# A written order for the mixer's projection on three engines, with x loaded ahead, a fifth gate tile as block products and forms moved behind the attention

## The chip, the cores and the metric

The kernel runs on one core of a Trainium2 chip. A core has TensorE (PE, matrix products into PSUM banks), VectorE (DVE), ScalarE (ACT), GpSimd (POOL), and DMA queues, of which the kernel uses SyncE's (SP) for nearly all loads and POOL's for loads that add to what is in the buffer. The metric is the device time of one execution in microseconds (us); the median of three runs counts.

## The reference

One layer on x of 512 x 1024 in float32. `D` is 1024, the tiles of 128 channels are numbered m or k.

```python
h = rms_norm(x, norm_mix)
q_a, k_a, v_a, u_b, gate_b, gate_c, g_a, g_b = jnp.split(h @ w_in, split_points, axis=-1)
o_a = stick_breaking_attention(heads(q_a), heads(k_a), heads(v_a))
y_b = gate_b * causal_depthwise_conv(gate_c * u_b, conv_w)
merged = sigmoid(g_a) * (o_a @ w_branch_a) + sigmoid(g_b) * (y_b @ w_branch_b)
x = x + merged @ w_mix_out
x = x + memory_cross_attention(rms_norm(x, norm_mem_q), rms_norm(mem, norm_mem_kv), ...)
gate, up = jnp.split(rms_norm(x, norm_ffn) @ w_ffn_in, 2, axis=-1)
x = x + (silu(gate) * up) @ w_ffn_out
return rms_norm(x, norm_final)
```

The change touches the sixth line from its gates on, and the seventh, with what the memory attention's query (memory-q) needs of its result.

## The kernel before

All activations lie transposed, channels on partitions and 512 positions along the row. Each float32 product is made of three products in a faster type: every operand is split into a high part, a cast on ACT (`wh`, `mh`, names ending in h), and a low part, a subtraction on DVE (`wl`, `ml`), and `mm3` issues high x high, high x low and low x high. A weight tile goes through `load_w`: a 512 KB load by SP into a buffer of the tag `wr`, the cast to `wh` on ACT, the subtraction to `wl` on DVE. **The tag `wr` has four buffers**, and so has each of `wh` and `wl`.

The larger weights are computed as seven *block products* in place of eight half products (`product(ps, m, i)`, i = 0 to 6, each with 12 matmuls 256 columns wide). Those need sums of weight blocks, which `ffn_load` makes: `ws` (a 512 KB load, then an accumulating load on POOL's queue), `wg` (512 KB) and `a22` (256 KB). `ws` and `wg` take buffers of the tag `wr` too, but for one of them at two of three tiles, which take the tag `wg` of another pool. `ffn_raw` adds further sums, `ffn_form` splits one into high and low (`wf`). On the side of the activations each pair of tiles is turned into *forms*: `xf`, `xo`, `xc`, `xd` with h and l behind, by `forms_of`, where c and d are differences of blocks.

The stages from about 150 us on:

- *Attention.* The stick-breaking attention on PE, ACT, DVE and POOL, its order left to the scheduler.
- *Gates, branches.* For each tile m the two gates (projections of h, a sigmoid each) and the two branch projections (`branch`: 12 + 12 matmuls into a bank `br`, each multiplied by its gate in place on DVE, then added to the merged tile `m`). In tiles 0 to 3 the gates are direct (24 matmuls, 512 wide, each); the last `GATES` = 4 tiles use block products, whose x forms are built pair by pair by `pair_load` and `pair_forms` (an xp load of 512 KB into a `wr` buffer, two scalings by ACT at line 776, then the sums). The last tiles run under a written order on PE, ACT and DVE: products by number, and at each the reads of its bank (`gate_reads`), the form of a product four ahead, the sum of one six ahead, and at i = 6 the branch. `gate_second` adds the second half of a gate; for the last tile it stands behind the product i = 5. `merged.append(split(...))` makes `mh` and `ml` of the merged tiles.
- *Mixer.* `residual(wmix_d, ...)`: for m = 0 to 7 one block of 24 matmuls (512 wide) into a bank `r`, drawn from two banks that `br` and `v` use as well; then the load of x (SP, 256 KB, line 622), the add x <- r + x (DVE, L625), the scaled `xr` (ACT, L628), at odd m the forms of the pair, and the squares for the next norm. Nothing sets the order here but the scheduler's priorities and the buffers.
- *Memory-q.* Block products again: `z`, `v`, `y` banks, in a written order whose head takes products 0 to 2 over the first three pairs first, then the fourth pair, then i = 3, 4 and so on.
- *The second residual* (`wmo_d`) and the FFN use the same code and forms.

SP carries out its loads in program order: a load whose buffer is not free holds those behind it.

Of the kernel before, what the change touches and what calls it, by code (L numbers as in the profile page):

```python
# [13 lines left out]
P = 128  # L14
D = 1024
S = 512
# [16 lines left out]
QM = NF + NB  # L33
GATES = 4
GM = QM + D // (2 * P)
# [12 lines left out]
def hybrid_layer(ctx: ExitStack, tc: tile.TileContext, xT_d, memT_d, cols_d, wv_d, win_d,  # L48
# [540 lines left out]

    def forms_of(xe, xo):  # L590

        b11 = xe[:, :HS]
        c, d = sums_of(xe, xo)
        u = unit("xf")
        nc.scalar.copy(u[:, :HS], b11)
        nc.vector.tensor_tensor(out=u[:, HS:], in0=b11, in1=f(u[:, :HS]), op=ALU.subtract)  # L596
        (oh, ol), (ch, cl), (dh, dl) = split(xo, "xo"), split(c, "xc"), split(d, "xd", new=spare)
        return listed((u[:, :HS], u[:, HS:]), oh, ol, ch, cl, dh, dl)

# [5 lines left out]
    def residual(w_dram, act, old, gain):  # L605


        xs, xn = [], []
        acc = tmp("acc")
        ps, w, even = {}, {}, {}  # L610

        def block(m, k0, k1, bank=mmtile):
            if k0 == 0:
                w[m] = load_w(w_dram[m])
# [3 lines left out]
            if k1 < KD:  # L618
                return
            if old is None:  # L620
                xm = f(unit("x"))
                nc.sync.dma_start(xm, xT_d[m * P:(m + 1) * P, :])
            else:
                xm = old[m]
            nc.vector.tensor_tensor(out=xm, in0=ps[m], in1=xm, op=ALU.add)  # L625
            xs.append(xm)
# [12 lines left out]

        return (xs, xn, acc), block  # L640

# [5 lines left out]

    raws, pairs = {}, {}

    def ffn_load(m):  # L650
# [101 lines left out]

    def branch(m, sig, w):
        for j, a in ((1, yb), (0, oT)):
            ps = mmtile("br")
            gemm(ps, w, a, 4 * j)
            nc.vector.tensor_tensor(out=sig[j], in0=ps, in1=sig[j], op=ALU.mult)
        t = f(spare("m"))
# [14 lines left out]
    def pair_forms(k2, xp):  # L773
        for j in range(2):
            k = 2 * k2 + j
            nc.scalar.activation(xp[:, j, :], xp[:, j, :], AF.Copy, scale=g_mix[:, k:k + 1])
# [4 lines left out]
    x0f = []  # L781
    for m in range(KD - GATES):
        sig = []
        for j in range(2):
# [3 lines left out]
            squash(sig[j])  # L788
        if m < KD // 2:
            xp = pair_load(m)  # L790
        branch(m, sig, load_w(wbr_d[m]))
        if m < KD // 2:
            x0f.append(pair_forms(m, xp))

# [34 lines left out]
    with tc.manual_schedule(engines={mybir.EngineType.PE, mybir.EngineType.Activation,  # L829
                                     mybir.EngineType.DVE}):  # L830
        wb, last_m = {}, GM + GATES - 1
        for n, (m, i) in enumerate(gs):
            product(bank_of(m, i), m, i)
            if i == 1 and m > GM:
                gate_second(m - 1)
            elif (m, i) == (last_m, 5):
                gate_second(m)
            gate_reads(m, i)
            if n + GATE_AHEAD < len(gs):
# [3 lines left out]
            if i == 3:  # L843
                wb[m] = load_w(wbr_d[KD - GATES + m - GM])
            if i == 6:
                b = banks.pop(m)
                branch(KD - GATES + m - GM, (b["g"], b["t"]), wb[m])
                sigmoid = b["sigmoid"]
            if m == last_m and i in (1, 2, 3, 4):
                merged.append(split(raw_m[len(merged)], "m"))  # L850
        while len(merged) < KD:
            merged.append(split(raw_m[len(merged)], "m"))

    (x1, x1f, acc1), mix = residual(wmix_d, merged, None, g_q)
# [127 lines left out]

    x2, last = residual(wmo_d, om, x1, g_ffn)
    with tc.manual_schedule(engines={mybir.EngineType.PE}):
# [117 lines left out]
    for k in range(TURN):  # L1102
# [3 lines left out]
        if k > 1 and k % 2 == 0 and len(af) < NT:  # L1106
            j = TURN + 2 * len(af)
            af.append(forms_of(act[j], act[j + 1]))
        for m in range(KD):
# [194 lines left out]
```

## Time and profile before

| | us |
|---|---|
| median of three runs (859.42 to 861.13) | 860.27 |
| the profiled execution | 858.25 |
| its span, first to last instruction | 856.4 |
| PE busy | 843.1 |
| DVE busy | 671.3 |
| ACT busy | 479.9 |
| POOL busy | 81.5 |

The mean granted clock of PE was 0.996 of full speed. In a row of the timeline stand the start in us from the span's start, the duration, the engine, the line, the operation, what is written from what with its shape, and in brackets how long the engine had been idle and what it waited for. A matmul's duration overlaps its neighbours'; what counts is the distance of starts. A row of waits reads: who waited, for whom, us in total, how often, the longest. A row of windows gives the stretch, its length, the busy share and count of PE, PE's weight loads, DVE, ACT and POOL, then the granted clock, the DMA share and GB/s.

### The profile page before, as it was taken

The page shows a single profiled execution, that of the slowest core. Times are in us where ns is not written, and L with a number is a line of the kernel's source. Part 1 is how long each engine was busy: PE and PEld are TensorE (multiplying, and loading weights), DVE is VectorE, ACT ScalarE, POOL GpSimd, SP SyncE. Part 2 cuts the span into 40 slices and gives each one's busy share as a digit, 9 for nine tenths or more (in the row PEclk, how much of TensorE's full clock was granted, in tenths as well). Part 3 has the DMA queues.
Part 4 walks back from the last instruction along what each step waited for, and adds up shares of the span by engine and source line. Part 5 has one row for each costly group of instructions (what it writes and reads, how often), then busy time and mean ns, then how long its engine had stood idle before and what let it go on. Part 6 is the DMA issues. An engine that isn't in the chain of part 4 may idle for free.

```text
span 856.4 us, 13976 instructions
## 1 busy us (share of the span) xinstructions
PE 843.1 (98%) x5344; PEld 762.5 (89%) x5344; DVE 671.3 (78%) x1169; ACT 479.9 (56%) x866; POOL 81.5 (10%) x106
## 2 busy tenths in 40 slices
PE   9999999999999999999999999999999999999997
PEld 7878787788899887899988889999999999888997
DVE  8769889888666967778865789888888878876864
ACT  7556766676344655566664666555554456652444
POOL 1011112111100001000000110111111110010002
PEclk9999999999999999999999999999999999999999
DMA  8332232217544745546332336777777775362312
GB/s 296 129 118 77 96 106 78 89 50 218 150 121 126 215 146 155 135 134 236 124 104 94 106 79 174 200 183 181 182 179 184 185 192 172 135 153 67 97 38 99
DMA packets 50483, 119.98 MB, mean 140 GB/s; under 512 B 5104, under 2 KB 9200, under 8 KB 50416
## 3 DMA queue, kind: packets, MB, share of 16 engines
q1 hardware_dynamic: 40880, 100.97, 36.1%
q0 software_dynamic: 9248, 17.83, 12.8%
q8 instruction: 42, 0.69, 0.3%
q10 hardware_dynamic: 288, 0.29, 0.1%
q14 instruction: 25, 0.20, 0.1%
HBM read 115.89 MB, written 2.10 MB: 138 GB/s over the span
## 4 chain that ended last, share of the span: by engine, by line
PE 90%; DVE 4%; issue 2%; DMA 2%; ACT 1%; POOL 0%; SPq 0%; DVEq 0%; POOLq 0%
PE z L706 22%; PE y L706 11%; PE v L706 5%; PE pr L162 5%; PE pr L164 5%; PE pr L163 5%; PE f L162 3%; PE f L163 3%; PE f L164 3%; PE v L268 3%; PE r L162 3%; PE r L163 3%; PE r L164 2%; PE br L163 2%; PE br L162 2%; PE br L164 2%
## 5 line engine op out<-in xcount | busy, mean ns | idle before, releaser
L157 ACT CAST wh<-wr 128x1024 fp32r<-128x1024 f32 x82 | 85.7, 1049 | 58.6 <-issue 9.7
L158 DVE TENSOR_TENSOR wl<-wr,wh 128x1024 fp32r<-128x1024 f32 x82 | 101.1, 1236 | 22.2 <-ACT wh L157 21.7
L706 PE MATMUL z<-xdh,wf 128*128 128x256 f32 x544 | 108.8, 284 | 0.0
L706 PEld LDWEIGHTS z<-xdh,wf 128*128 128x128 f32 x544 | 89.3, 191 | 0.3
L162 PE MATMUL pr<-xgh,wh 128*128 128x512 f32 x224 | 87.7, 391 | 0.0
L163 PE MATMUL pr<-xgl,wh 128*128 128x512 f32 x224 | 87.4, 390 | 0.0
L164 PE MATMUL pr<-xgh,wl 128*128 128x512 f32 x224 | 87.3, 390 | 0.0
L706 PE MATMUL z<-xdl,wf 128*128 128x256 f32 x272 | 77.1, 283 | 0.0
L730 ACT COPY sa<-z 128x256 f32<-128x256 f32 x52 | 19.4, 373 | 86.4 <-PE z L706 86.3
L697 DVE TENSOR_TENSOR wf<-s,wf 128x512 fp32r<-128x512 f32 x68 | 46.8, 689 | 24.5 <-ACT wf L696 23.3
L696 ACT CAST wf<-ws 128x512 fp32r<-128x512 f32 x68 | 41.8, 618 | 32.3 <-PE r L163 10.0
L688 DVE TENSOR_TENSOR wf<-wg,wf 128x1024 fp32r<-128x1024 f32 x34 | 41.6, 1224 | 21.4 <-ACT wf L687 21.3
L663 POOL DMA_DIRECT2D ws<-in_w_ffn_in_dram x22 | 26.5, 1203 | 306.0 <-DMA ws<-in_w_ffn_in_dram 133.1
L697 DVE TENSOR_TENSOR wf<-ws,wf 128x512 fp32r<-128x512 f32 x68 | 46.9, 690 | 10.8 <-ACT wf L696 10.7
L706 PE MATMUL y<-xch,wf 128*128 128x256 f32 x272 | 54.6, 282 | 0.0
L706 PE MATMUL z<-xch,wf 128*128 128x256 f32 x272 | 54.5, 283 | 0.0
L706 PEld LDWEIGHTS z<-xdl,wf 128*128 128x128 f32 x272 | 52.0, 191 | 0.2
L696 ACT CAST wf<-s 128x512 fp32r<-128x512 f32 x68 | 42.3, 622 | 15.5 <-DVE s L674 14.8
L706 PE MATMUL z<-xf,wf 128*128 128x256 f32 x360 | 48.9, 284 | 1.4 <-DVE xf L596 0.9
L164 PEld LDWEIGHTS pr<-xgh,wl 128*128 128x128 f32 x224 | 42.0, 188 | 8.8
L162 PEld LDWEIGHTS pr<-xgh,wh 128*128 128x128 f32 x224 | 42.1, 188 | 8.6 <-DVE rv L131 0.3
L163 PEld LDWEIGHTS pr<-xgl,wh 128*128 128x128 f32 x224 | 42.1, 188 | 8.3
(327 smaller groups left out, 2453.3 us busy)
## 6 DMA issues: line engine op xcount, KB each, us to landing
wr<-in_w_in_dram SPq DMA_DIRECT2D x28, 512.0 KB, 3.5
ws<-in_w_ffn_in_dram SPq DMA_DIRECT2D x22, 512.0 KB, 4.0
ws<-in_w_ffn_in_dram POOLq DMA_DIRECT2D x22, 512.0 KB, 6.0
wg<-in_w_ffn_in_dram SPq DMA_DIRECT2D x22, 512.0 KB, 4.5
wr<-in_w_ffn_out_dram SPq DMA_DIRECT2D x14, 512.0 KB, 3.5
a<-in_w_ffn_in_dram SPq DMA_DIRECT2D x22, 256.0 KB, 4.8
wr<-in_w_branch_dram SPq DMA_DIRECT2D x8, 512.0 KB, 3.9
wr<-in_w_mix_out_dram SPq DMA_DIRECT2D x8, 512.0 KB, 5.0
```

Source lines behind the costliest of these rows:

```text
L157: after(nc.scalar.copy(h2, raw), lead[-1:])
L158: lows.append(nc.vector.tensor_tensor(out=l2, in0=raw, in1=f(h2), op=ALU.subtract))
L162: nc.tensor.matmul(ps, a[0], b[0], start=start, stop=False, **kw)
L163: nc.tensor.matmul(ps, a[0], b[1], start=False, stop=False, **kw)
L164: nc.tensor.matmul(ps, a[1], b[0], start=False, stop=stop, **kw)
L268: nc.tensor.matmul(vps[t], xg[k][a][:, sl], wv[k][b], start=k == 0 and (a, b) == (0, 0), stop=k == KD - 1 and a == 1)
L663: nc.gpsimd.dma_start(s13, a[:, 0:4:3, :], accum_op=ALU.add)
L688: nc.vector.tensor_tensor(out=lo, in0=pair, in1=f(hi), op=ALU.subtract)
L696: nc.scalar.copy(hi, raw)
L697: nc.vector.tensor_tensor(out=lo, in0=raw, in1=f(hi), op=ALU.subtract)
L706: nc.tensor.matmul(ps[:, :HS], a, b, start=i < 3 and k == 0 and j == 0, stop=k == KP - 1 and j == 2, skip_group_check=True)
L730: nc.scalar.copy((s[:, :HS], None, None, s[:, HS:], t[:, :HS], t[:, :HS])[i], z)
```

## The change

- `GATES` goes from 4 to 5: the fourth direct gate tile becomes block products. The pair forms are made one after each of three direct branches, the fourth with the third.
- The scalings in `pair_forms` are tied behind the attention's exponentials.
- `forms_of` is cut into `even_forms` (what needs the even tile alone) and `odd_forms`, which write the same forms in another order; the residuals and the FFN use them.
- The mixer's projection comes under the written order on PE, ACT and DVE, 24 matmuls to a block; the weight of m + 2 is asked for before the last matmuls of block m, and its cast and subtraction stand there. The weight of m = 0 is asked for at the last gate tile's product 5.
- The eight loads of x are written at the last gate tile's product 6, and the `ws` loads that follow are tied behind them.
- The last gate tile's `gate_second` goes from i = 5 to i = 4. Its branch takes splits of merged tiles, and the weight of m = 1, between its matmuls and its mults (`also`).
- Memory-q's raw weights are asked for ahead of the mixer, and six of its forms are made within it, at m = 5, 6 and 7.

```diff
-GATES = 4
+GATES = 5
...
+    def even_forms(xe):
+        u, c = unit("xf"), f(unit("c1"))
+        nc.scalar.copy(u[:, :HS], xe[:, :HS])
+        nc.vector.tensor_tensor(out=c[:, :HS], in0=xe[:, :HS], in1=xe[:, HS:], op=ALU.subtract)
+        nc.vector.tensor_tensor(out=u[:, HS:], in0=xe[:, :HS], in1=f(u[:, :HS]), op=ALU.subtract)
+        return u, c, xe
+
+    def odd_forms(u, c, xe, xo):
...
+        nc.scalar.copy(ch, c)
+        nc.vector.tensor_tensor(out=ol, in0=xo, in1=f(oh), op=ALU.subtract)
...
+        nc.scalar.copy(dh, d)
+        nc.vector.tensor_tensor(out=cl, in0=c, in1=f(ch), op=ALU.subtract)
+        nc.vector.tensor_tensor(out=dl, in0=d, in1=f(dh), op=ALU.subtract)
...
+        def finish(m):
+            xm = old[m]
             nc.vector.tensor_tensor(out=xm, in0=ps[m], in1=xm, op=ALU.add)
...
             if m % 2:
-                xn.append(forms_of(even.pop(m - 1), raw))
+                xn.append(odd_forms(*even.pop(m - 1), raw))
             else:
-                even[m] = raw
+                even[m] = even_forms(raw)
...
-        nc.sync.dma_start(s13, a[:, 2:3, :].broadcast_to([P, 2, 512]))
+        after(nc.sync.dma_start(s13, a[:, 2:3, :].broadcast_to([P, 2, 512])), x_loads[-1:])
...
-    def branch(m, sig, w):
+    def branch(m, sig, w, also=()):
         for j, a in ((1, yb), (0, oT)):
             ps = mmtile("br")
             gemm(ps, w, a, 4 * j)
+            for g in also[j:j + 1]:
+                g()
             nc.vector.tensor_tensor(out=sig[j], in0=ps, in1=sig[j], op=ALU.mult)
...
-            nc.scalar.activation(xp[:, j, :], xp[:, j, :], AF.Copy, scale=g_mix[:, k:k + 1])
+            after(nc.scalar.activation(xp[:, j, :], xp[:, j, :], AF.Copy,
+                                       scale=g_mix[:, k:k + 1]), exps[-2:])
...
+            if (m, i) == (last_m, 4):
                 gate_second(m)
...
+            if (m, i) == (last_m, 5):
+                mix_all, mix, mix_w = residual(wmix_d, merged, x1, g_q)
+                mix_w(0)
             if i == 6:
+                if m == last_m:
+                    for k in range(KD):
+                        x1.append(f(unit("x")))
+                        x_loads.append(nc.sync.dma_start(x1[k], xT_d[k * P:(k + 1) * P, :]))
                 b = banks.pop(m)
-                branch(KD - GATES + m - GM, (b["g"], b["t"]), wb[m])
+                branch(KD - GATES + m - GM, (b["g"], b["t"]), wb[m],
+                       (lambda: (merge(1), mix_w(1)), lambda: merge(2)) if m == last_m else ())
...
-    for m in range(KD):
-        mix(m, 0, KD)
-
-    qs = order(QM, MH)
-    for n in range(AHEAD + SUM_AHEAD):
-        ffn_raw(*qs[n], nc.gpsimd)
-    for n in range(AHEAD):
-        ffn_form(*qs[n])
+        qs = order(QM, MH)
+        for n in range(AHEAD + SUM_AHEAD):
+            ffn_raw(*qs[n], nc.gpsimd)
+        for m in range(KD):
+            mix(m, 0, KD - 1)
+            if m + 2 < KD:
+                mix_w(m + 2)
+            mix(m, KD - 1, KD)
+            for n in {5: (0, 2), 6: (3, 4), 7: (5,)}.get(m, ()):
+                ffn_form(*qs[n])
```

Three places show how the engines' orders move. First SP's queue, at the mixer's weights, before (`wr` from in_w_mix_out are the mixer's weights, `ws`, `wg` and `a` memory-q's):

```order
L150 DMA wr_3164<-in_w_mix_out_dram 128x1024
L662 DMA a_3525<-in_w_mem_q_dram 128x512
L150 DMA wr_3224<-in_w_mix_out_dram 128x1024
L150 DMA wr_3263<-in_w_mix_out_dram 128x1024
L150 DMA wr_3323<-in_w_mix_out_dram 128x1024
L150 DMA wr_3362<-in_w_mix_out_dram 128x1024
L150 DMA wr_3422<-in_w_mix_out_dram 128x1024
L150 DMA wr_3461<-in_w_mix_out_dram 128x1024
L622 DMA x_3158<-in_xT_dram 128x512
L658 DMA ws_3521<-in_w_mem_q_dram 128x2x512
```

and with the change:

```order
L150 DMA wr_3203<-in_w_mix_out_dram 128x1024
L681 DMA a_3220<-in_w_mem_q_dram 128x512
L883 DMA x_3148<-in_xT_dram 128x512
L883 DMA x_3162<-in_xT_dram 128x512
L677 DMA ws_3216<-in_w_mem_q_dram 128x2x512
L677 DMA ws_3225<-in_w_mem_q_dram 128x2x512
L679 DMA wg_3227<-in_w_mem_q_dram 128x1024
L677 DMA ws_3705<-in_w_mem_q_dram 128x2x512
L681 DMA a_3229<-in_w_mem_q_dram 128x512
L150 DMA wr_3254<-in_w_mix_out_dram 128x1024
L150 DMA wr_3294<-in_w_mix_out_dram 128x1024
L150 DMA wr_3347<-in_w_mix_out_dram 128x1024
```

(six more loads of x stand between the two shown). Before, all eight weights of the mixer stood ahead of x and of most of memory-q's raws; now those of m = 2 to 7, from wr_3254 on, stand behind them, and `ws_3216`, `ws_3225` and `wg_3227` are in buffers of the tag `wr`.

Second, DVE at the end of the last gate tile and the start of the mixer, with the change (`sb` and `fg` are the gates, `br` the branch banks, `m` the merged tiles):

```order
L836 SCALAR_TENSOR_TENSOR sb_2924<-z_2923,r0b_338 128x256
L158 TENSOR_TENSOR wl_3130<-wr_3127,wh_3129 128x1024
L840 TENSOR_TENSOR fg_2937<-y_2982,fg_2937 128x256
L841 TENSOR_TENSOR fg_2937<-fg_2937,r0b_338 128x512
L177 TENSOR_TENSOR ml_3178<-m_2731,mh_3177 128x512
L177 TENSOR_TENSOR ml_3182<-m_2899,mh_3181 128x512
L778 TENSOR_TENSOR sb_2924<-br_3164,sb_2924 128x512
L177 TENSOR_TENSOR ml_3200<-m_3109,mh_3199 128x512
L158 TENSOR_TENSOR wl_3206<-wr_3203,wh_3205 128x1024
L778 TENSOR_TENSOR fg_2937<-br_3186,fg_2937 128x512
```

Before, the two mults of that branch (L757 there) followed the r0b mult at once, and the last four ml stood behind them.

Third, DVE in the mixer's second half, with the change (wl_3445 and wl_3487 are the weights of m = 6 and 7, x_3156 and x_3158 the adds of m = 4 and 5, x_3160 that of m = 6):

```order
L158 TENSOR_TENSOR wl_3445<-wr_3442,wh_3444 128x1024
L645 TENSOR_TENSOR x_3156<-r_3420,x_3156 128x512
L593 TENSOR_TENSOR c_3455<-xr_3452 128x256
L594 TENSOR_TENSOR xf_3454<-xr_3452,xf_3454 128x256
L657 TENSOR_TENSOR acc_3126<-acc_3126,sq_3459 128x512
L158 TENSOR_TENSOR wl_3487<-wr_3484,wh_3486 128x1024
L645 TENSOR_TENSOR x_3158<-r_3462,x_3158 128x512
L603 TENSOR_TENSOR c_3455<-xr_3494,xr_3452 128x256
L604 SCALAR_TENSOR_TENSOR c_3496<-c_3455,xr_3494 128x256
```

```order
L716 TENSOR_TENSOR wf_3519<-ws_3216,wf_3519 128x512
L645 TENSOR_TENSOR x_3160<-r_3522,x_3160 128x512
```

The adds and forms of m now stand behind the weight of m + 2, and those of m = 6 also behind two of memory-q's weight forms.

More of the change, by code (lines that the diff above doesn't have):

```diff
@@ L588, in sums_of, with act_forms @@
         return c, d
[L590 to L598, printed above, removed]
+    def even_forms(xe):
[5 more added lines that the diff above has]
+    def odd_forms(u, c, xe, xo):
+        lo, hi = slice(0, HS), slice(HS, S)
+        d = f(unit("c2"))
+        oh, ol, ch, cl = (unit(t) for t in ("xoh", "xol", "xch", "xcl"))
+        dh, dl = spare("xdh"), spare("xdl")
+        nc.scalar.copy(oh, xo)
+        nc.vector.tensor_tensor(out=c[:, hi], in0=xo[:, hi], in1=xe[:, hi], op=ALU.subtract)
+        nc.vector.scalar_tensor_tensor(out=d[:, lo], in0=c[:, lo], scalar=-1.0, in1=xo[:, hi],
+                                       op0=ALU.mult, op1=ALU.subtract)
+        nc.scalar.copy(ch, c)
+        nc.vector.tensor_tensor(out=ol, in0=xo, in1=f(oh), op=ALU.subtract)
+        nc.vector.scalar_tensor_tensor(out=d[:, hi], in0=d[:, lo], scalar=-1.0, in1=xo[:, lo],
+                                       op0=ALU.mult, op1=ALU.subtract)
+        nc.scalar.copy(dh, d)
+        nc.vector.tensor_tensor(out=cl, in0=c, in1=f(ch), op=ALU.subtract)
+        nc.vector.tensor_tensor(out=dl, in0=d, in1=f(dh), op=ALU.subtract)
+        return listed((u[:, lo], u[:, hi]), oh, ol, ch, cl, dh, dl)
+    def act_forms(k2):
+        return odd_forms(*even_forms(act[k2]), act[k2 + 1])
     def listed(first, oh, ol, ch, cl, dh, dl):
@@ L646, in hybrid_layer @@
     FORM_TAGS = "wh", "wl"
-    raws, pairs = {}, {}
+    raws, pairs, x_loads = {}, {}, []
     def ffn_load(m):
@@ L788, in hybrid_layer @@
             squash(sig[j])
-        if m < KD // 2:
-            xp = pair_load(m)
         branch(m, sig, load_w(wbr_d[m]))
-        if m < KD // 2:
-            x0f.append(pair_forms(m, xp))
+        gate_pair(m)
+    for k2 in range(KD - GATES, KD // 2):
+        gate_pair(k2)
     def gate_reads(m, i):
@@ L831, in hybrid_layer, with merge @@
         wb, last_m = {}, GM + GATES - 1
+        x1 = []
+        def merge(n):
+            for _ in range(n):
+                merged.append(split(raw_m[len(merged)], "m"))
         for n, (m, i) in enumerate(gs):
@@ L981, in mem_out @@
             om.append(split(ps, "om"))
-    x2, last = residual(wmo_d, om, x1, g_ffn)
+    x2, last, _ = residual(wmo_d, om, x1, g_ffn)
     with tc.manual_schedule(engines={mybir.EngineType.PE}):
@@ L1107, in hybrid_layer @@
             j = TURN + 2 * len(af)
[L1108 removed]
+            af.append(act_forms(j))
         for m in range(KD):
```

31 lines of the change are left out of this document (14 added, 17 removed).

## The prediction

> **What bounds the kernel now.** I read the page's engines and its chain of waits first, then who PE waited for.
>
> ```profile
> PE 843.1 (98%) x5344; PEld 762.5 (89%) x5344; DVE 671.3 (78%) x1169; ACT 479.9 (56%) x866; POOL 81.5 (10%) x106
> PE 90%; DVE 4%; issue 2%; DMA 2%; ACT 1%; POOL 0%; SPq 0%; DVEq 0%; POOLq 0%
> ```
>
> TensorE (PE) is busy for 843.1 of 856.4 us. A change pays only by taking matmuls out or by closing one of these gaps:
>
> ```profile
> PE r L162 <- DVE x L625: 1.7, 1, 1.7
> PE y L706 <- DVE xcl L177: 1.2, 2, 0.6
> PE z L706 <- DVE xf L596: 0.9, 1, 0.9
> PE z L440 <- ACT l L376: 0.6, 1, 0.6
> PE z L706 <- ACT xf L595: 0.6, 1, 0.6
> PE y L706 <- DVE sb L822: 0.5, 1, 0.5
> ```
>
> All six lie where the change works: the first in the mixer, then the forms behind the two residuals, the attention, the last gate tile. What the gaps behind the mixer cost beyond their length is in the windows by microsecond, whose third number from the end is the granted clock (PEclk):
>
> ```profile
> 354.00:355.00 1.00, 0.42 (x4) 0.26 (x2) 1.00 (x4) 1.00 (x2) 0.00 (x0) 1.00 0.88 309
> 355.00:356.00 1.00, 1.00 (x6) 0.90 (x6) 1.00 (x3) 0.03 (x1) 0.76 (x1) 0.61 0.49 172
> 356.00:357.00 1.00, 1.00 (x7) 1.00 (x7) 1.00 (x3) 0.00 (x0) 0.44 (x1) 0.50 0.17 55
> 357.00:358.00 1.00, 1.00 (x6) 1.00 (x6) 0.42 (x1) 0.00 (x0) 0.00 (x0) 0.50 0.84 45
> 358.00:359.00 1.00, 1.00 (x8) 1.00 (x7) 0.03 (x1) 0.89 (x2) 0.00 (x0) 0.68 0.86 164
> ```
>
> The clock is halved for (0.39+0.5+0.5+0.32)x2 = 3.4 us, which loses 1.7 us of matmuls. The anchors on PE, from its timeline:
>
> ```profile
> 301.27 0.39 PE L162 MATMUL r<-mh,wh 128*128 128x512 f32 x1
> 335.99 0.47 PE L162 MATMUL r<-mh,wh 128*128 128x512 f32 x1 [1.73 <-DVE x L625]
> 340.19 0.39 PE L162 MATMUL r<-mh,wh 128*128 128x512 f32 x1
> 346.77 0.39 PE L164 MATMUL r<-mh,wl 128*128 128x512 f32 x1
> 346.99 1.24 PE L706 MATMUL z<-xf,wf 128*128 128x256 f32 x9
> 348.07 0.28 PE L706 MATMUL v<-xoh,wf 128*128 128x256 f32 x1
> 358.89 0.28 PE L706 MATMUL z<-xch,wf 128*128 128x256 f32 x1
> ```
>
> From 340.19 to 346.77 are 29 steps: a 512-wide matmul costs 0.2267 us. Nine 256-wide products take 348.07 - 346.99: 0.12 each. The mixer (192 matmuls, 43.5 us) runs from 301.27 to 346.99, 45.7 us. From there to the fifth of memory-q's seven products, at 358.89, lie 60 products, 7.2 us of work in 11.9: 4.7 lost, 1.7 of it to the clock.
>
> **The change part by part.**
>
> *Fifth gate tile.* 48 matmuls x 0.2267 = 10.88 go, 84 products x 0.12 = 10.08 come: **-0.8**. Block products now start 10.9 us earlier, which asks for their weights earlier:
>
> ```profile
> 221.54 1.21 POOL L663 DMA_DIRECT2D ws<-in_w_gates_dram  x1 [17.55 <-DVE c L583]
> 231.27 0.62 ACT L696 CAST wf<-ws 128x512 fp32r<-128x512 f32 x1 [7.49 <-DMA ws<-in_w_gates_dram]
> ws<-in_w_gates_dram POOLq DMA_DIRECT2D x4, 512.0 KB, 8.2
> ```
>
> The accumulating DMA took 9.7 us (8.2 in the median). Its buffer comes free with an early pair form; I put its issue near 211.3 (an estimate, from DVE's order and the pair forms' rows). The casts and the sum behind it must be through by some 223.1, and fit if it lands by 219.9. At 8.2 (219.5) no stall, at 9.7 about 1.5; I take **+0.4**, ends 0 and 1.5.
>
> *Attention.* The scaling of x pairs leaves ACT's queue ahead of the attention's casts:
>
> ```profile
> 158.33 1.33 ACT L776 ACTIVATE xp<-xp,gcol 128x512 f32<-128x512 f32 x2 [2.60 <-DMA xp<-in_xT_dram]
> 159.57 0.36 ACT L403 ACTIVATE e<-z 128x256 f32<-128x256 f32 x1
> 163.17 0.40 ACT L376 CAST l<-e 128x256 fp32r<-128x256 f32 x1 [0.50 <-POOL e L362]
> ```
>
> Waiting for its xp it delayed e by more than the 0.6 that PE then waited for l; the branch's ol, made just behind the attention, comes earlier too: **-0.7** (ends 0 and -0.8).
>
> *Last gate tile.* The late sb add goes one product earlier: **-0.5**.
>
> *Into the mixer.* The first r block takes the bank that the last branch's first mult frees. That mult now stands on DVE behind two splits (ml) of `merge(2)`, whose second cast on ACT stands behind the table load:
>
> ```profile
> 294.90 0.63 ACT L763 ACTIVATE sb<-sb 128x512 f32<-128x512 f32 x1
> 298.73 0.60 ACT L176 CAST mh<-m 128x512 fp32r<-128x512 f32 x1
> 299.35 1.28 ACT L116 ACT_TABLE_LOAD   x1
> 301.28 1.06 ACT L157 CAST wh<-wr 128x1024 fp32r<-128x1024 f32 x1 [0.65 <-issue]
> 294.46 0.41 DVE L811 SCALAR_TENSOR_TENSOR sb<-sb,r0b 128x256 f32<-128x256 f32 x1
> 294.79 1.22 DVE L158 TENSOR_TENSOR wl<-wr,wh 128x1024 fp32r<-128x1024 f32 x1
> 296.00 0.42 DVE L815 TENSOR_TENSOR fg<-y,fg 128x256 f32<-128x256 f32 x1
> 297.48 0.68 DVE L816 TENSOR_TENSOR fg<-fg,r0b 128x512 f32<-128x512 f32 x1
> 298.82 0.69 DVE L757 TENSOR_TENSOR sb<-br,sb 128x512 f32<-128x512 f32 x1 [0.66 <-ACT fg L763]
> ```
>
> Say PE is through with the branch at T0. The z product behind which all this hangs ends at T0-6.88 (then 12 products and 24 matmuls). Behind it follow, some 0.2 apart or overlapped by 0.1: two L811-like operations (0.8), sigmoid and wh (1.6), wl (1.2), y add and r0b mult (1.1), sigmoid (0.6), mh (0.6), table load (1.3), mh (0.6), ml (0.6), mult (0.7). They sum to 9.1 to 9.3, so r may start at **T0+2.45** (ends 1.5, if each hand-over is quick, and 3.2). No PE work is left to hide it.
>
> *Mixer.* x asked for ahead of time takes out the wait at 335.99: -1.88 of pitch, with 0.3 of small ones. But memory-q's ws, ws and wg now hold three of the four wr buffers through the whole mixer, and weights m=2 to 7 all go through the fourth: each load waits on SP for the wl two tiles before it.
>
> ```profile
> wr<-in_w_in_dram SPq DMA_DIRECT2D x28, 512.0 KB, 3.5
> wr<-in_w_mix_out_dram SPq DMA_DIRECT2D x8, 512.0 KB, 5.0
> 335.15 0.69 DVE L625 TENSOR_TENSOR x<-r,x 128x512 f32<-128x512 f32 x1 [1.41 <-DMA x<-in_xT_dram]
> 512.08 0.68 DVE L177 TENSOR_TENSOR xcl<-c,xch 128x512 fp32r<-128x512 f32 x1
> ```
>
> A link is 3.5 landing + wh 1.05 + wl 1.22 + 0.1 = 5.9 us, with 0.6 more on two links whose cast stands behind ACT's forms; a block on PE takes 24 x 0.2267 = 5.44. Counted from the mixer's start the first link starts at 1.7, so wl of m=7 ends at 1.7 + 6x5.9 + 1.2 = 38.2, when PE has just reached that block (7x5.44 = 38.1). PE loses about **0.8** in m=6 and 7: 44.3 us. With what went, the stage from 301.27 costs 2.45 + 44.3 - 45.7 = **+1.0**. The lower end of a link is 3.4 landing; the upper, 5.0, is a rival below.
>
> *Behind the mixer.* On DVE, wl of m+2 stands ahead of the x add of m (the third place of the order above). The add of m=5, ready at 33.0, therefore runs at 38.1. Behind it DVE has nine forms (5.2 us by pitches of 0.34 for 256 columns, 0.6 for 512, 1.14 for 1024, and 1.3 waiting for ACT's casts), so the add of m=6 comes at 45.2, after the mixer's end, and that of m=7, behind another five and the wf pair, at 50.2; the last form (xdl) ends at 54.7 and ACT's casts at 55.3. The fourth product so starts at 55.4 and the fifth 18 products later, at 57.5: 13.2 us after the mixer, 6.0 lost where before 3.0 went without the clock: +3.0. PE idles for 6 of 8 us there, so I keep one window of half clock at 1.7 (ends 0 and 3.4): **+3.0**.
>
> > The Trainium skill, "TensorE: Matmul & The Clock Gate", section "Part 1: The HAM clock gate", has the clock halved after an idle window of about 3.4 us, free-running, and at full only again after a busy one. The 3.4 us of half clock above agree; that they followed gaps of at most 0.9 us does not. By its rule no gap foreseen here is long enough, which is the second rival.
>
> *Second residual.* xcl there (512.08) is formed before xdl now, so most of PE's second wait of 0.6 for xcl goes: **-0.6** (ends 0 and -0.7). ACT's and DVE's other moved forms lie beside matmuls; SP's loads for memory-k come after the late links but are wanted some 50 us on.
>
> *Sum:* -0.8 + 0.4 - 0.7 - 0.5 + 1.0 + 3.0 - 0.6 = **+1.8**. On the profiled 858.25 (span 856.4 and 1.85 around it) that gives 860.05; the profiled execution stands 2.0 below the runs' median, 860.27, so **862.1** on the median.
>
> **Rivals.**
>
> *The weights come in time* (a buffer is free sooner than I read, or the loads land at 3.0). Then DVE is not pushed back, the adds come at each block's end, and PE has 33 products (4.0 us) to cover the last add and xoh (some 2.7 us): about 1 lost in the head, no half clock, and no 0.8. The sum falls by 0.8 + 5.0 + 1.7 = 7.5: 854.6, or up to 858 when only half of it holds. For it: every price here is within 0.5 us a link of PE's own pace. Against: the buffers are counted, four.
>
> *No half clock* after the longer gaps: at 335.99 a gap of 1.73 had none behind it. 862.1 - 1.7 = 860.4, no change.
>
> *Slow links.* Mix weights took 5.0 us in the median when other loads ran beside them, as x, memory-q and their accumulations do at the mixer's start. At 5.0 a link takes 7.4, wl of m=7 ends at 1.7 + 6x7.4 = 46.1, and PE ends at 51.6, 7.3 later: 869. It decides from a link over 5.9, so part of it (865) is likelier than all.
>
> *The gate tile is not cheaper*, with a stall of 1.5 for its accumulation: 863.2, inside the forecast.
>
> **How the numbers follow.** The forecast 0.42 (860.5 to 864.5 by itself), weights in time 0.25, no half clock 0.18, slow links 0.15. 0.2% is 1.7 us. Faster: the first rival and 0.02 of the second, 0.27. Same: 0.16 of the second and 0.12 of the forecast, whose lower part lies under 862.0: 0.28. Slower: 0.30 and 0.15. The range leaves out the far parts of the first and third rival: 855.5 to 867.
>
> **What would show it.** Right: PE waiting some 2.4 us ahead of the first r matmul for a mult on DVE with ml ahead of it; loads of mix weights one at a time, some 5.9 us apart, each after a wl; DVE idle in the mixer with wh as releaser; x adds of m=5 to 7 late; 13 us between the mixer's end and memory-q's fifth product, with PEclk at 0.5; no wait for l, sb or xT. Wrong: mix weights issued in a bunch, x adds at each block's end, or a first r that follows the branch at once. A loss in the gates ahead of 300 us would be the accumulation's.

## The result, and the profile after

| | before | after | |
|---|---|---|---|
| median of 16 runs each, us | 858.66 | 861.79 | |
| ratio, with its 95% interval | | 1.0054 | 1.0036 to 1.0073 |
| the profiled execution, us | 858.25 | 861.28 | |
| its span, us | 856.4 | 859.4 | +3.0 |
| PE busy, us | 843.1 | 845.0 | +1.9 |

The change makes the kernel slower by 0.5%, 4.6 us by the ratio. The profiled execution lies near its median; five of the 16 runs took 865.9 to 867.9 us and the others 859.7 to 863.5, which is where the ratio's further 1.6 us come from. PE is busy for longer although its matmuls cost less than before: busy time counts matmuls at half clock too.

Who PE waited for, in the changed kernel (engine, line and tile; for whom; us in all, times, longest):

```profile
PE r L162 <- DVE sb L778: 2.9, 1, 2.9
...
PE v L725 <- ACT xoh L602: 0.9, 1, 0.9
PE br L162 <- DVE g L314: 0.8, 1, 0.8
PE z L725 <- DVE wf L707: 0.8, 1, 0.8
PE z L725 <- issue: 0.6, 1, 0.6
PE v L725 <- DVE xol L607: 0.4, 1, 0.4
...
```

The waits of before are gone: for x, for l, for the late sb add, for xf and for xcl. New ones stand in their place, and the first, ahead of the mixer, is the largest of either kernel. On PE's timeline, the last matmul of the branches, the first of the mixer, the first and the fifth product of memory-q:

```profile
299.15 0.39 PE L164 MATMUL br<-oh,wl 128*128 128x512 f32 x1
302.40 0.77 PE L162 MATMUL r<-mh,wh 128*128 128x512 f32 x1 [2.87 <-DVE sb L778]
...
348.85 1.24 PE L725 MATMUL z<-xf,wf 128*128 128x256 f32 x9
...
362.43 0.41 PE L725 MATMUL z<-xch,wf 128*128 128x256 f32 x1
```

With the distance of a matmul's starts, 0.23, the branches end at 299.38. In stages, with the prediction's terms:

| from, to | before | after | change | predicted |
|---|---|---|---|---|
| start, first branch | 199.93 | 198.53 | -1.4 | -0.7 |
| first branch, end of branches | 101.34 | 100.85 | -0.5 | -0.9 |
| end of branches, first block of the mixer | 0.0 | 3.02 | +3.0 | +2.45 |
| mixer | 45.72 | 46.45 | +0.7 | -1.4 |
| mixer's end, memory-q's fifth product | 11.90 | 13.58 | +1.7 | +3.0 |
| fifth product, second residual | | | +0.2 | 0 |
| second residual to the end | | | -0.8 | -0.6 |
| sum | | | +3.0 | +1.8 |

The mixer has no wait in it and still takes 46.45 us for 43.5 us of matmuls. The windows show why (length; busy share and count of PE, weight loads, DVE, ACT, POOL; granted clock, DMA share, GB/s):

```profile
300.00:302.00 2.00, 0.00 (x0) 0.00 (x0) 1.51 (x2) 1.93 (x3) 1.10 (x1) 0.89 0.95 252
302.00:304.00 2.00, 1.60 (x4) 1.34 (x5) 2.00 (x4) 0.00 (x0) 0.00 (x0) 0.50 1.08 259
304.00:306.00 2.00, 2.00 (x7) 1.52 (x6) 1.28 (x2) 0.59 (x1) 0.00 (x0) 0.50 1.06 398
306.00:308.00 2.00, 2.00 (x6) 1.61 (x5) 0.69 (x1) 0.16 (x2) 1.20 (x1) 0.50 0.49 199
308.00:310.00 2.00, 2.00 (x9) 1.60 (x8) 1.06 (x1) 0.91 (x1) 0.00 (x0) 0.91 0.79 103
...
356.00:358.00 2.00, 1.74 (x5) 1.20 (x5) 1.92 (x5) 1.57 (x4) 0.00 (x0) 0.54 0.00 0
358.00:360.00 2.00, 1.55 (x7) 1.58 (x8) 2.00 (x5) 1.39 (x4) 0.00 (x0) 0.50 0.00 0
360.00:362.00 2.00, 2.00 (x11) 2.00 (x10) 1.71 (x3) 0.61 (x2) 0.00 (x0) 0.50 0.76 246
362.00:364.00 2.00, 2.00 (x15) 2.00 (x15) 1.10 (x2) 1.17 (x3) 0.58 (x1) 0.75 0.85 260
```

The clock is halved twice, each time for 6.8 us (the missing shares summed and doubled: (0.22 + 3.0 + 0.18) x 2 and (0.92 + 1 + 1 + 0.5) x 2), where before had one stretch of 3.4 (the half clock in the program's last microseconds, which every run has, left aside). From the mixer's first matmul at 302.40 on that loses 2.9 us of matmuls.

How the adds of x lag, on DVE (wl is the weight of m = 7, the x adds those of m = 5, 6 and 7), and SP's issue of the mixer's weights:

```profile
339.95 1.23 DVE L158 TENSOR_TENSOR wl<-wr,wh 128x1024 fp32r<-128x1024 f32 x1 [1.58 <-ACT wh L157]
341.10 0.69 DVE L645 TENSOR_TENSOR x<-r,x 128x512 f32<-128x512 f32 x1
348.17 0.69 DVE L645 TENSOR_TENSOR x<-r,x 128x512 f32<-128x512 f32 x1
353.22 0.68 DVE L645 TENSOR_TENSOR x<-r,x 128x512 f32<-128x512 f32 x1
```

```profile
304.02 31.66 SPq L150 DMA_DIRECT2D wr<-in_w_mix_out_dram  x6
```

Six loads one at a time, in 31.66 us: 6.3 from one issue to the next. Each took 3.5 us in the median, as the view of the DMA issues over that stretch has it (count, size, us to landing), and each of the six had to wait until a subtraction `wl` set its buffer free (SP's own waits, 300 to 340 us):

```profile
wr<-in_w_mix_out_dram SPq DMA_DIRECT2D x6, 512.0 KB, 3.5
```

```profile
SPq L150 <- DVE wl L158: 19.6, 6, 6.0
```

Block 5 ended at 348.85 - 2 x 5.44 = 338.0; its add ran at 341.1, 3.1 us later; that of block 6 (343.4) at 348.2, 4.8 later; that of block 7 at 353.2, 4.4 us after the mixer. This is what the prediction described.

### The profile page after: what moved, and what is told of

It is laid out like the page before. It is cut to its first block, busy times and chain, and to the rows that moved or that the text cites. A ratio compares the mean times of both kernels' runs of the same rounds, so it can differ in the third digit from the quotient of the medians.

```text
span 859.4 us, 14074 instructions
## 1 busy us (share of the span) xinstructions
PE 845.0 (98%) x5380; PEld 766.0 (89%) x5380; DVE 677.7 (79%) x1179; ACT 484.3 (56%) x873; POOL 83.5 (10%) x107
## 4 chain that ended last, share of the span: by engine, by line
PE 89%; DVE 3%; ACT 3%; DMA 2%; issue 1%; POOL 0%; SPq 0%; DVEq 0%; ACTq 0%; POOLq 0%
PE z L725 23%; PE y L725 11%; PE v L725 6%; PE pr L162 5%; PE pr L163 5%; PE pr L164 5%; PE f L163 3%; PE f L164 3%; PE f L162 3%; PE r L162 2%; PE v L268 2%; PE r L163 2%; PE r L164 2%; PE z L440 1%; PE o L468 1%; PE br L162 1%
## 5 line engine op out<-in xcount | busy, mean ns | idle before, releaser
L158 DVE TENSOR_TENSOR wl<-wr,wh 128x1024 fp32r<-128x1024 f32 x80 | 97.5, 1221 | 30.8 <-ACT wh L157 28.4
L725 PE MATMUL z<-xdh,wf 128*128 128x256 f32 x560 | 112.1, 284 | 0.6 <-issue 0.6
L725 PEld LDWEIGHTS z<-xdh,wf 128*128 128x128 f32 x560 | 91.9, 191 | 1.1 <-issue 0.9
L162 PE MATMUL pr<-xgh,wh 128*128 128x512 f32 x208 | 81.5, 392 | 0.0
L163 PE MATMUL pr<-xgl,wh 128*128 128x512 f32 x208 | 81.2, 390 | 0.0
L164 PE MATMUL pr<-xgh,wl 128*128 128x512 f32 x208 | 81.1, 390 | 0.0
L715 ACT CAST wf<-s 128x512 fp32r<-128x512 f32 x70 | 43.5, 622 | 25.7 <-DVE s L693 16.4
L725 PE MATMUL v<-xoh,wf 128*128 128x256 f32 x240 | 48.7, 284 | 0.9 <-ACT xoh L602 0.9
L162 PE MATMUL f<-acth,wh 128*128 128x512 f32 (+1 forms) x144 | 49.3, 342 | 0.0
L163 PE MATMUL f<-actl,wh 128*128 128x512 f32 (+1 forms) x144 | 49.2, 342 | 0.0
L164 PE MATMUL f<-acth,wl 128*128 128x512 f32 (+1 forms) x144 | 49.2, 342 | 0.0
```

The costliest lines, as they stand in the source:

```text
L158: lows.append(nc.vector.tensor_tensor(out=l2, in0=raw, in1=f(h2), op=ALU.subtract))
L162: nc.tensor.matmul(ps, a[0], b[0], start=start, stop=False, **kw)
L163: nc.tensor.matmul(ps, a[0], b[1], start=False, stop=False, **kw)
L164: nc.tensor.matmul(ps, a[1], b[0], start=False, stop=stop, **kw)
L715: nc.scalar.copy(hi, raw)
L725: nc.tensor.matmul(ps[:, :HS], a, b, start=i < 3 and k == 0 and j == 0, stop=k == KP - 1 and j == 2, skip_group_check=True)
```

## The experiments

The theory (below: the weight chain) has two parts. The mult behind the splits makes a gap ahead of the mixer; and the mixer's weights, which go through one buffer because memory-q's raws hold the other three, drive DVE so late that the stretch up to memory-q's fifth product ends when the last weights allow, whatever happens ahead of it. The rival takes the gap, or the order of the forms on DVE, for the loss. All kernels are compared by the time from the end of the branches to that fifth product, called the *stretch* here, since the waits ahead of 240 us differ from run to run. It is read from the one profiled execution of each kernel.

| run | from the changed kernel, or from before | ratio to before, 95% interval | stretch, us |
|---|---|---|---|
| before | | 1 | 57.62 |
| changed | | 1.0054 (1.0036 to 1.0073) | 63.05 |
| e1 | mult ahead of the splits | 1.0059 (1.0035 to 1.0082) | 61.98 |
| e2 | raws behind block 3 | 1.0006 (0.9995 to 1.0018) | 60.75 |
| e3 | e1 and e2 | 1.0014 (0.9997 to 1.0031) | 59.84 |
| e4 | gap filled | 1.0042 (1.0030 to 1.0055) | 62.82 |
| e5 | four gate tiles | 1.0061 (1.0044 to 1.0078) | 64.15 |
| e6 | e1, raws behind block 5 | 0.9953 (0.9937 to 0.9969) | 55.23 |
| e7 | e6, four gate tiles | 0.9954 (0.9938 to 0.9969) | 56.70 |
| e8 | before, x asked for early | 0.9941 (0.9928 to 0.9954) | 51.94 |
| e9 | mixer left to the scheduler | 0.9913 (0.9889 to 0.9936) | 50.93 |
| e10 | e9, four gate tiles | 0.9907 (0.9891 to 0.9922) | 50.97 |
| e11 | e9, scalings not tied | 0.9911 (0.9891 to 0.9932) | 50.95 |
| e12 | e9, pairs in turn | 0.9870 (0.9851 to 0.9890) | 50.96 |

### e1: the mult ahead of the splits

```diff
-            for g in also[j:j + 1]:
-                g()
+            if j == 0:
+                for g in also[:1]:
+                    g()
             nc.vector.tensor_tensor(out=sig[j], in0=ps, in1=sig[j], op=ALU.mult)
+            if j == 1:
+                for g in also[1:]:
+                    g()
```

> The last branch's first mult stands on DVE ahead of the two splits of merge(2), nothing else changes. Both theories expect the wait of the first r matmul (2.87 us) to fall under 1 us and the half clock from 302.4 to 308.2 to go, so that PE reaches its first blocks some 5.5 us earlier. Theory of the weight chain: the weights of m = 2 to 7 come through one buffer, a link of some 5.9 us each, and their start (the wl of m = 1) moves by about 1 us only; so PE waits for weights or adds later in the mixer and behind it, and memory-q's fifth product starts only 1 to 1.5 us earlier than in the changed kernel: ratio to before about 1.004. Rival, the gap is a plain loss: the whole 5.5 us come out at the end, ratio about 0.998 to 0.999.

The gap is gone (the first r starts with the end of the branches) and so is its half clock, and the stretch is 1.07 us shorter, as the weight chain has it; the rival's 5.5 us do not come. PE waits inside the mixer instead, now that it is there earlier than the weights and splits:

```profile
PE br L162 <- DVE g L314: 2.7, 1, 2.7
...
PE pr L162 <- DVE g L779: 1.5, 1, 1.5
PE r L162 <- ACT mh L176: 1.1, 1, 1.1
PE r L162 <- DVE x L645: 0.9, 2, 0.8
...
```

The ratio is no better than the changed kernel's. In this profile the two waits for g, ahead of 240 us, make 4.2 us, in the changed one 0.8.

### e2 and e3: memory-q's raws behind block 3

```diff
-        for n in range(AHEAD + SUM_AHEAD):
-            ffn_raw(*qs[n], nc.gpsimd)
         for m in range(KD):
             mix(m, 0, KD - 1)
             if m + 2 < KD:
                 mix_w(m + 2)
+            if m == 3:
+                for n in range(AHEAD + SUM_AHEAD):
+                    ffn_raw(*qs[n], nc.gpsimd)
```

> Memory-q's raw weights are asked for behind block m = 3 of the mixer and not ahead of it, so that the mixer's weights up to m = 5 go through four buffers. Theory of the weight chain: the gap ahead of the mixer and its half clock stay (5.9 us), but the wl of m = 7 ends some 4 to 6 us earlier against the block's start, the adds of m = 5 and 6 run within 1 to 2 us of their block's end, and the stretch from the mixer's end to memory-q's fifth product falls from 13.6 to some 10 us: ratio about 1.000 to 1.001. Rival, the adds are late because of the order of the forms on DVE and not because of weights: no more than 1 us, ratio about 1.004.

> Both edits. Theory of the weight chain: gap, half clock and late adds go together, 8 to 9 us less than the changed kernel: ratio 0.995 to 0.997. If the gap is a plain loss and the weights cost nothing: as the first kernel, 0.998. If only the order on DVE counts: no better than the better of the two alone.

e2's ratio came out, 4 us better than the changed kernel with the gap left in, but not by the way that was expected. The stretch is only 2.3 us shorter: 0.5 in the gap, 1.2 in the mixer, whose half clock lasted 3.4 us and not 6.8, and 0.6 in the head, which took 12.96 us and not 10. The rest of the ratio lies outside the stretch: none of e2's 11 runs is over 862, where five of the changed kernel's 16 are over 865. The last wl starts 38.3 us after the branches' end (338.45 - 300.19; 40.6 in the changed kernel). Against the start of its block it ends 0.6 us earlier than there, not 4 to 6, and the adds of m = 5 and 6 are still 2.5 and 4.1 us late. (The wait rows of e2 and e5 name a cast, wh, ahead of the first r and not the mult; the first r starts 0.15 us after the mult's end in all three kernels, so the mult still fits as what held it.)

e3 missed: the stretch fell to 59.84 and not to some 54. Its DVE rows for the weights of m = 5, 6 and 7 show what was left:

```profile
326.47 1.98 DVE L158 TENSOR_TENSOR wl<-wr,wh 128x1024 fp32r<-128x1024 f32 x1 [0.25 <-ACT wh L157]
335.64 1.23 DVE L158 TENSOR_TENSOR wl<-wr,wh 128x1024 fp32r<-128x1024 f32 x1 [2.11 <-ACT wh L157]
341.51 1.22 DVE L158 TENSOR_TENSOR wl<-wr,wh 128x1024 fp32r<-128x1024 f32 x1 [1.58 <-ACT wh L157]
```

Asked for behind block 3, the raws take their buffers ahead of the weights of m = 6 and 7, which are one link behind the other again, in e2 as in e3: e3's last wl starts 37.8 us after the branches' end (341.51 - 303.74), 40.6 in the changed kernel.

### e4: the gap filled with matmuls

```diff
+        hold = ztile("hold")
+        for _ in range(12):
+            nc.tensor.matmul(hold, neg1, neg1[:, None, :].broadcast_to([P, S // P, P]), start=True,
+                             stop=True)
         merge(KD - len(merged))
```

> Twelve matmuls that compute nothing (512 wide, into a bank of their own) fill the 3 us ahead of the first r matmul; the wait on DVE stays. If the half clock from 302.4 to 308.2 comes from that gap, PE keeps full clock there and the mixer's end comes 2.5 to 3 us earlier; by the theory of the weight chain the adds of m = 5 to 7 then still run when they did, so that memory-q's fifth product gains less than 1 us (ratio 1.004 to 1.005); if the chain does not bind, all 2.9 us come out (ratio 1.002). If the clock has another cause, the half clock stays and nothing moves.

The first r starts as late as in the changed kernel, with a wait of 0.17 us in place of 2.87, and the clock stays full (PE's timeline, and the windows over the mixer's start):

```profile
302.76 0.47 PE L162 MATMUL r<-mh,wh 128*128 128x512 f32 x1 [0.17 <-DVE sb L778]
...
336.21 0.47 PE L162 MATMUL r<-mh,wh 128*128 128x512 f32 x1 [0.53 <-DVE x L645]
...
362.50 0.28 PE L725 MATMUL z<-xch,wf 128*128 128x256 f32 x1
```

```profile
302.00:305.00 3.00, 2.83 (x13) 2.04 (x12) 2.96 (x6) 0.24 (x1) 0.00 (x0) 1.00 1.07 287
305.00:308.00 3.00, 3.00 (x15) 2.49 (x14) 1.37 (x2) 0.62 (x1) 1.02 (x1) 1.00 0.81 322
```

So idling halved the clock there. The mixer ends 1.28 us earlier (347.57), part of the gain going into a new wait for an x add, and the fifth product starts at 362.50 where it started at 362.43: next to nothing of it arrives, 0.2 us in the stretch. The chain sets that time.

### e5: four gate tiles

```diff
-GATES = 5
+GATES = 4
```

> The change with four gate tiles as block products again, the rest as it is. In the changed kernel and the kernels made from it PE waited 0.8 to 4.3 us ahead of 240 us (br and pr for g on DVE), with ACT waiting for the third x pair's load. Theory, the fifth tile's loads and forms crowd there: these waits fall under 0.5 us in all; the direct tile costs 0.8 more; from the first r on nothing changes (63 us from the last branch's end to memory-q's fifth product). Net 0 to 3 us less than the changed kernel, ratio 1.002 to 1.005, and less spread between runs. Rival, the waits come from the tie of the scalings behind the attention: they stay, and the ratio is 1.006.

The theory of this run fell. PE still waits 1.0 us there (pr for g), the ratio is the rival's, 1.006, and one run of six is some 3 us above the rest here too. In e10, with four tiles, the same wait is 2.6 us. What ACT stands at in these two is a load too, but of a direct gate's weight (2.0 and 2.2 us in e5, 3.6 in e10), with a cast of pair forms behind it. The stretch, 64.15, is 1.1 longer than the 63 expected. The rival's cause, the tie, fell as well: e11 has no tie and waits 0.8 us for g.

### e6 and e7: all weights through four buffers

As e3, with `m == 5` for `m == 3`; e7 with `GATES = 4` too.

> The mult ahead of the splits, and memory-q's raws asked for behind block m = 5, so that all eight weights of the mixer go through four buffers. Theory of the weight chain: in the run with both edits the weights of m = 6 and 7 were still two links behind each other; without them wl of m = 7 ends before block 6 does, the adds of m = 5, 6 and 7 run within 1.5 us of their block's end, and from the last branch's end to memory-q's fifth product pass 53 to 55 us (59.8 with both edits, 63.0 in the changed kernel, 57.6 before): ratio 0.993 to 0.996 if the waits ahead of 240 us are as long as they were there. Rival, the order of forms on DVE makes the adds late by itself: 58 us or more, ratio 1.000.

> As the kernel before this one, with four gate tiles. If the fifth tile costs more by its waits than its 0.8: ratio 1 to 3 us below that kernel's, 0.991 to 0.994. If the tile is a gain as such: 0.8 us above it.

This is the weight chain undone: 4.0 us under before by the ratio, where the changed kernel was 4.6 above. From e1, whose edit it has too, it differs only in when memory-q's raws are asked for, and that takes 6.8 us out of the stretch (61.98 to 55.23). No run gave the tag more buffers; that the buffers bind is read from SP's six waits for wl in the changed kernel. The last wl starts 33.7 us after the branches' end (298.74). The add of m = 5 runs 1.2 us after its block (344.03 - 10.88 = 333.2), those of m = 6 and 7 run 2.9 and 2.5 us after, where 1.5 was expected:

```profile
332.48 1.99 DVE L158 TENSOR_TENSOR wl<-wr,wh 128x1024 fp32r<-128x1024 f32 x1 [0.25 <-ACT wh L157]
334.39 0.68 DVE L645 TENSOR_TENSOR x<-r,x 128x512 f32<-128x512 f32 x1
341.46 0.68 DVE L645 TENSOR_TENSOR x<-r,x 128x512 f32<-128x512 f32 x1
346.51 0.68 DVE L645 TENSOR_TENSOR x<-r,x 128x512 f32<-128x512 f32 x1
```

The adds of m = 6 and 7 still stand behind memory-q's weight forms, and the stretch, 55.23, is a little over the 53 to 55 expected: of the 12 us that the changed kernel is above e9 some 8 go with the gap and the chain, and 4.3 stay with the written order. e7 does not tell the gate tile's worth: the two ratios are the same, though its profile is worse in the stretch, where 3.4 us of half clock came back.

### e8: x asked for early, alone

To the kernel before:

```diff
+    x1 = []
+    for k in range(KD):
+        x1.append(f(unit("x")))
+        nc.sync.dma_start(x1[k], xT_d[k * P:(k + 1) * P, :])
-    (x1, x1f, acc1), mix = residual(wmix_d, merged, None, g_q)
+    (x1, x1f, acc1), mix = residual(wmix_d, merged, x1, g_q)
```

> The kernel before with one thing changed: the eight loads of x stand ahead of the mixer. If the wait for x in the mixer was a loss that x asked for early gives back: 1.5 to 1.9 us less, ratio 0.998, no wait of r for the x add. Rival, the loads of x take the place of memory-q's, which come later: the mixer gains 1.9 and the stretch behind it loses as much, ratio 1.000.

Both expectations were too small: 5.1 us come out, not 1.9. PE's waits there are these, but for the start, none of them in the mixer or behind it but one for xcl (the row counts two, the other being at the second residual):

```profile
PE y L706 <- DVE xcl L177: 1.2, 2, 0.6
PE y L706 <- DVE sb L822: 0.5, 1, 0.5
PE br L162 <- ACT oh L176: 0.5, 1, 0.5
PE z L440 <- ACT l L376: 0.4, 1, 0.4
PE br L163 <- DVE ol L177: 0.2, 1, 0.2
```

The mixer takes 43.66 us, and the stretch behind it 8.28 in place of 11.90, at full clock. Of before's 4.7 us lost behind the mixer 3.6 went with this edit too: the last x add ran 2.4 us after its block's end (349.37 against 346.99), here 0.2 after (346.01 against 345.81). The scheduler also set another order of the forms; the two were not taken apart.

### e9, e10, e11: the rest of the change without its written order

e9 is the changed kernel with the mixer as before: no `also`, the splits behind the branch, and after the written part

```diff
+    (x1, x1f, acc1), mix, _ = residual(wmix_d, merged, x1, g_q)
+    for m in range(KD):
+        mix(m, 0, KD)
+
+    qs = order(QM, MH)
+    for n in range(AHEAD + SUM_AHEAD):
+        ffn_raw(*qs[n], nc.gpsimd)
+    for n in range(AHEAD):
+        ffn_form(*qs[n])
```

e10 has `GATES = 4` with it, e11 no tie of the scalings to the attention's exponentials.

> The change without its written order for the mixer: x asked for early, five gate tiles, the scalings behind the attention, the cut forms and the earlier sb add stay; the blocks of the mixer, the splits ahead of it, the mixer's weights and memory-q's raws go back to the scheduler's order. Theory, the written order with memory-q's raws ahead of the mixer's weights is the whole loss: from the last branch's end to memory-q's fifth product pass 52 us as in the run with x early alone (63.0 in the changed kernel), the 0.7 at the second residual and the 1.4 ahead of the branches stay: 4 us below the run with x early alone less what PE waits ahead of 240 us (0.8 to 4.3): ratio 0.988 to 0.993. Rival, the fifth tile, the tie and the forms are losses too: above 0.994.

> The same with four gate tiles. If the fifth tile's waits ahead of 240 us outweigh its 0.8: 0.5 to 3 us below the kernel before this; if not, 0.8 above.

> The kernel with five tiles and the scheduled mixer, its scalings of x pairs not tied behind the attention. If the tie gave the 1.4 us ahead of the first branch, the first branch starts at 199.5 to 200 again and not at 198, and the third pair's scaling still waits for its load: 1 to 1.5 us above the tied kernel. If the tie only moves the wait for x pairs to the gates: no difference, with the waits of PE ahead of 240 us shorter by as much as the attention is longer.

e9 settles what the written order costs: 1.4% less than the changed kernel, 12 us, at full clock but for the program's last 4 us. The stretch is 50.93 us, of which 50.7 are matmuls. PE's waits in the whole program, but for the start:

```profile
PE br L162 <- DVE g L314: 0.8, 1, 0.8
```

The ratios of e9, e10 and e11 overlap, so neither the fifth tile nor the tie can be told from nothing by the runs. The first branch starts at 198.6, 198.5 and 198.2, with and without the tie, and at 199.9 in before and e8. So the 1.4 us there do not need the tie. But the wait in ACT's queue that the tie was to remove is gone in e11 too: before, the first scaling waits 2.60 us for its load ahead of the attention's exponentials (158.33); in e11 the scheduler put it behind a cast `l` of the attention, at 161.04, and it waits for nothing.

### e12: the pairs in turn

In e9 two of six runs were 4 to 5 us longer. ACT's rows of the changed kernel show a queue that e9 has as well: the scaling of the fourth x pair waits for its load with the cast of the first pair, which DVE and a branch's mult need, behind it.

```profile
206.81 0.72 ACT L797 ACTIVATE xp<-xp,gcol 128x512 f32<-128x512 f32 x1 [1.63 <-DMA xp<-in_xT_dram]
207.44 0.60 ACT L176 CAST xdh<-c 128x512 fp32r<-128x512 f32 x1
```

```diff
             after(nc.scalar.activation(xp[:, j, :], xp[:, j, :], AF.Copy,
-                                       scale=g_mix[:, k:k + 1]), exps[-2:])
+                                       scale=g_mix[:, k:k + 1]),
+                  exps[-2:] + (casts[-1:] if k2 > 1 else []))
```

> The kernel with five gate tiles and the scheduled mixer, and the scalings of x pairs 2 and 3 tied behind the last cast of the pair ahead of them, so that ACT no longer stands at pair 3's load with that cast (xdh of pair 0) queued behind it. Theory, this wait is what PE pays ahead of 240 us and what differs between runs: PE's waits there fall from 0.8 (up to 4.3 in other kernels with five tiles) to under 0.3, the runs that are 4 to 5 us longer (two of six) no longer occur, and the median is 848 to 849: ratio 0.987 to 0.990. Rival, the waits and the spread come from the gates' own weights (wg and the accumulating load): median and spread as they were, ratio 0.991.

The four runs took 846.9 to 847.7 us, 1.3% less than before, and PE waits for nothing but the constant of the program's first matmuls:

```profile
PE warm L227 <- DVE neg L94: 1.6, 1, 1.6
```

That the wait for the pair's load was the cause of PE's waits is shown. That it also made the long runs is likely and no more: six runs of e9 and four of e12 are few. One profile speaks for it. The profiled execution of e3, 861.82 us, is one of its four runs over 861; the other eight took 857.6 to 859.5. There ACT stands 3.9 us at that load, where it was 1.6 in the changed kernel's profile, and PE's two waits for g make 4.3 us, with 3.4 us of half clock behind them (223 to 227 us):

```profile
208.38 0.72 ACT L801 ACTIVATE xp<-xp,gcol 128x512 f32<-128x512 f32 x1 [3.92 <-DMA xp<-in_xT_dram]
```

## Why the prediction was right

**Right: the direction, the time (862.1 against 861.79) and the mechanisms.** The first r waited for the mult behind ml, as worked out (3.02 us by starts; 2.45 said, where the working's own terms make 2.2 to 2.4; the difference is a second ml of 1.16 us, 1.09 to the next start where 0.6 was counted, and a hand-over. In e2 and e5, where that ml took 0.69, it is 2.55 and 2.54). Mix weights came one at a time. Counted from the mixer's start, the wl of m = 7 ended at 38.8 (38.2 said) and the adds of m = 5 to 7 ran at 38.7, 45.8 and 50.8 (38.1, 45.2 and 50.2 said). The stretch behind the mixer took 13.6 us (13.2 said, and 1.7 for the clock), and no wait for x, for l or for the late sb add was left. e1, e4 and e6 show that the weight chain and not the gap decides.

**The change itself was forecast too small: +1.8, measured +3.0 in the profile and +4.6 by the ratio.** That the time fits so well is partly luck, since the base, 860.27 in the runs that were shown, was 858.66 in 16 runs. These terms were mis-sized:

- *Into the mixer.* The step priced the gap and put the clock behind it at nothing; half clock was counted in one place only, behind the mixer, and the one row on a longer gap ("at 335.99 a gap of 1.73 had none behind it") was used for the rival there. The gap of 2.87 halved the clock for 6.8 us, 2.9 us of matmuls. Its length could not have told: gaps of 2.67 and 2.63 us in e1 and e10 had none behind them.
- *Mixer.* "PE loses about 0.8 in m=6 and 7" did not come: by its gap and half clock PE was 2 us behind the weights. e1, with PE early, does wait there, 0.76 and 0.19 us at the start of blocks 6 and 7, but for x adds that stand behind a wl and not for the weights themselves.
- *Behind the mixer.* +3.0 said, +1.7 measured, for the same reason: since PE ended the mixer late against the chain, less of the lateness was left. The half clock lasted twice the one stretch that was counted.
- *Attention.* -0.7 said, -1.4 measured. The traces bear out the cause, a scaling that waits for its load in ACT's queue: counted from the attention's first matmul at line 440, before and the changed kernel are level up to 85.8 us and 1.2 us apart at 102.2, in the stretch where the first scaling stands in before (158.33 us of the span, ACT idle 2.60 ahead of it). PE's wait for l is 0.6 of that; what makes the other 0.6 was not taken apart. The last 0.2 of the 1.4 lies ahead of the attention, where the profiles of all kernels differ by up to 1.1 us. e11, level with the changed kernel, shows that the tie is one way to get this and not needed.
- *Fifth gate tile.* The stall was looked for at the accumulating load. It came from x pair loads in ACT's queue, 0.8 us of PE's time in the profile and up to 4.3 in others with five tiles; by e7 and e10 against e6 and e9 the tile's own gain is below what the runs tell.
- *x early* was counted as 1.9 in the mixer; alone it is worth 5.1 (4.0 to 6.2 by its interval), since the waits and the half clock behind the mixer went with it. The written order cost 12 us (e9 against the changed kernel), and so more than all of it.

The rivals: *weights in time* was sized about right, 6.8 us in the stretch from e1 to e6 where 7.5 was worked out, but needs another kernel. *No half clock* went the other way: two stretches of 6.8 us, where one of 3.4 was counted. *Slow links* did not come: the loads took 3.5 us in the median.

> On the clock, the Trainium skill, "TensorE: Matmul & The Clock Gate", section "Part 1: The HAM clock gate", gives windows of about 3.4 us, free-running. Every stretch of half clock in these profiles is 3.4 or 6.8 us long, but for the one at each program's end; that agrees. Its rule that the clock falls after an idle window of that length does not: 2.87 us sufficed, and the section "HAM oscillation — how this bites in real kernels" would have called this gap safe.

## What to carry to other kernels

Count the buffers of a tag over the whole stretch in which a written order asks for them: a prefetch that takes the buffers of a stream turns that stream into a chain of load, cast and subtraction, and its price shows far behind, where the forms are late. A gain on the busiest engine arrives only if the chain behind it moves too (e1 and e4 brought PE to the mixer's end 2.2 and 1.6 us earlier, counted from the branches' end, and of that 1.1 and 0.2 arrived), so change the pieces in pairs before judging either. And before writing an order by hand, give the scheduler the one thing that it lacked, here the loads of x, and see what is left to gain.

## What the runs showed of the hardware

- The length of a gap on PE did not tell whether the clock fell. A gap of 2.87 us was followed by 6.8 us of half clock, gaps of 2.39 in e2, 2.38 in e5 and 2.18 in e3 by 3.4; but gaps of 2.67 in e1 (ahead of 221.65), 2.63 in e10 (ahead of 212.20) and 1.73 in before by none. Three gaps of 0.57 to 0.87 us within 3.7 us were followed by 3.4 in before; behind the mixer, gaps of 0.31 to 0.90 at much the same distances were followed by 3.4 in e7 and by none in e6.
- Matmuls in the gap that compute nothing kept the clock full: granted 1.00 in e4 where it was 0.50 in the changed kernel.
- A subtraction of 128x512 on DVE took 1.16 us ahead of the mixer in the changed kernel and 1.22 in e4, 0.69 at the same place in e2 and e5, and some wl 1.98 to 2.33 us (1.23 elsewhere); why was not looked into.
